# Two tiles move from an eight-bank product to seven-block pairs, and its weights' lows come from adding DMAs

## The chip, the cores and the metric

The kernel runs on one core of one Trainium2 chip. The metric is device time in microseconds (us) of one execution. Engines go by these names: TensorE (PE in the profile; PEld is its weight load), VectorE (DVE), ScalarE (ACT), GpSimd (POOL) and SyncE (SP), which here issues nearly all DMAs.

## The reference

Two pre-norm residual layers over 512 tokens of 1024 features in float32: layer 0 with two kinds of full attention, layer 1 with neighbourhood attention and a relative-position bias. Each is followed by the MLP that this case is about:

```python
def sq_relu_mlp(h, w_up, w_down):
    u = jax.nn.relu(h @ w_up)
    return (u * u) @ w_down
...
for layer in range(DEPTH):                       # DEPTH = 2
    ...
    h = h + sq_relu_mlp(rmsnorm(h, norm_ffn[layer]), ffn_w_up[layer], ffn_w_down[layer])
return rmsnorm(h, final_norm)
```

`w_up` is 1024 x 4096 and `w_down` 4096 x 1024, so the hidden layer has 32 tiles of 128 features by 512 tokens.

## The kernel before

**Three matmuls for one.** A float32 product is made of three matmuls in TensorE's faster 32-bit format: each operand is split into a high part (its rounding, written by ScalarE) and a low part (the operand minus the high part, written by VectorE), and high x high, high x low and low x high are added (`mm3`). So a chunk of weights is loaded by SyncE into a raw buffer, ScalarE writes its high part (`whi`), VectorE its low part (`wlo`). There are 4 raw buffers, 3 high and 3 low ones. Each is 128 x 1024.

**The down product of an MLP** sums over the 32 hidden tiles. `SIZES` says for each MLP how they are divided: (6, 10, 14, 2) in MLP 0 and (6, 10, 12, 4) in MLP 1.
- The first 6 go through a plain product.
- The next 10 go through `product8`: all eight PSUM banks are in use, the loop over weight chunks (one chunk of 128 x 1024 for each hidden tile) is outside, the eight output tiles are inside. The first two chunks are run in two groups of four banks, the last two bank by bank so that banks come free one after another. A chunk is 8 x 3 = 24 matmuls of 512 columns.
- The next 14 (or 12) are kept raw and taken in pairs. `Seven` multiplies 2 x 2 blocks with seven block products for eight (Strassen's way): a chunk is 256 KB of weights, GpSimd makes three block sums of it (`seven_chunk`, L326 to L328), ScalarE the high part (L332) and VectorE the low part (L333), and TensorE runs 7 x 3 = 21 matmuls of 256 columns (L418 to L420). The product runs over four output groups of two tiles (`m`), in each over all pairs: 4 x 7 = 28 chunks in MLP 0, 24 in MLP 1. After each group the blocks are combined by ScalarE and VectorE (L426 to L430) and added to the residual (L1543).
- The last 2 (or 4) go through a plain product again.

The raw pairs' own block sums and their high and low parts (`convert`: `u7.sums`, `u7.split`; VectorE L360, L363, L388, L392, ScalarE L387) are made while `product8` runs, spread over its steps by the counter `at`. In MLP 0 the bias tables of layer 1 are written to HBM in the same place: `bias_rows`, 48 small DMAs (L1457 to L1463), one `next(bias, None)` for each step.

**The order of the weights' work.** Every chunk is planned in a list (`asked`). `weights(i)`, called when TensorE's chunk `i` is about to be emitted, starts the loads of chunks up to `i + LOAD` (5 ahead) and the high and low parts up to `i + AHEAD` (2 ahead). A chunk's steps are a generator: load, then high part, then low part. The three block sums of a `seven_chunk` follow its load directly. A `seven_chunk` takes a slot of the big pool in place of a raw buffer when more than `reserve[0]` slots are free; the pool has `NSLOT` slots of 128 x 1024. `reserve[0]` is 3 in the up product, `NSLOT` (no slots) while `product8` runs, then 1. A scheduler of the framework arranges the emitted instructions on each engine; instructions of one engine start in that order.

Of the kernel before, what the change touches and what calls it, by code (L numbers as in the profile page):

```python
# [8 lines left out]
F32 = mybir.dt.float32  # L9
# [9 lines left out]
P = 128  # L19
# [1 line left out]
FF = 4 * D  # L21
EPS = 1e-6
NEG = -1e30
NSLOT = 30
ROWS = 8
COLS = 64
C_ID, C_I1, C_I2, C_ROPE = 0, 128, 178, 182
# [8 lines left out]
def encoder_kernel(ctx: ExitStack, tc: tile.TileContext, ins, out, dbg=None):  # L36
# [167 lines left out]
    def chunk(parts, nk, ncol, heads=None, eng=None, first=False):  # L204

        raw = wp.tile([P, 1024], F32, tag="raw", bufs=4, name=nm("raw"))
        r3 = raw[:, 0 : nk * ncol].rearrange("p (k n) -> p k n", k=nk)
        for lo, n, src in parts:
            dst = r3[:, :, lo : lo + n]
            if len(src.shape) == 3:  # L210
                SP.dma_start(dst, src)
            else:
                for k in range(nk):
                    SP.dma_start(dst[:, k].rearrange("p (z m) -> p z m", z=src.shape[2]), src[:, k])
        yield
        hi = wp.tile([P, 1024], F32R, tag="whi", name=nm("whi"))
        lo_ = wp.tile([P, 1024], F32R, tag="wlo", name=nm("wlo"))
        m = nk * ncol
        v = lambda t: t[:, 0:m].rearrange("p (k n) -> p k n", k=nk)
        lows = []  # L220

        def low(to, src, high):
            z = lambda: (eng or DVE).tensor_tensor(to, src, f32(high), op=ALU.subtract)  # L223
            if eng:
                z()
            else:
                lows.append(z)

        if heads is None:
            if first:  # L230
                DVE.tensor_copy(hi[:, 0:m], raw[:, 0:m])
            else:
                ACT.activation(hi[:, 0:m], raw[:, 0:m], AF.Copy)  # L233
            low(lo_[:, 0:m], raw[:, 0:m], hi[:, 0:m])
        else:

            na, nb = heads
            hn = ncol // (na + nb)
            r4 = r3.rearrange("p k (h e) -> p k h e", h=hn)
            for e0, n, o in ((0, na, 0), (na, nb, hn * na)):  # L240
                z = [v(t)[:, :, o : o + hn * n].rearrange("p k (h e) -> p k h e", h=hn) for t in (hi, lo_)]
                src = r4[:, :, :, e0 : e0 + n]
                ACT.activation(z[0], src, AF.Copy)
                low(z[1], src, z[0])
        yield v(hi), v(lo_), lows

    def rows(w, k0, nk):
        return w[k0 * P : (k0 + nk) * P, :].rearrange("(k p) n -> p k n", p=P)


    asked, loaded, ready, low_parts = [], [], [], []
    AHEAD, LOAD = 2, 5

    def plan(*spec, make=None):
        asked.append((make or chunk, spec))
# [2 lines left out]
    def preload(n):  # L258
        while len(loaded) < min(n, len(asked)):
            make, spec = asked[len(loaded)]  # L260
            loaded.append(make(*spec))
            next(loaded[-1])

    def weights(i, ahead=AHEAD):
        preload(i + LOAD + 1)
        while len(ready) < min(i + ahead + 1, len(asked)):
            hi, lo, lows = next(loaded[len(ready)])
            ready.append((hi, lo))
            low_parts.append(lows)

            give_low(len(ready) - fixed[0])
        give_low(i + 1)
        return ready[i]
# [45 lines left out]
    def seven_chunk(w, k0, c0):  # L319


        slot = Slot(F32) if len(free) > reserve[0] else None
        raw = slot.t if slot else wp.tile([P, 1024], F32, tag="raw", bufs=4, name=nm("raw"))
        SP.dma_start(raw[:, 0:512].rearrange("p (k n) -> p k n", k=2), rows(w, k0, 2)[:, :, c0 : c0 + 256])
        r = raw.rearrange("p (b n) -> p b n", n=P)
        POOL.tensor_tensor(r[:, 6], r[:, 0], r[:, 1], op=ALU.subtract)  # L326
        POOL.tensor_tensor(r[:, 4:6], r[:, 2:3].to_broadcast([P, 2, P]), r[:, 0:7:6], op=ALU.add)  # L327
        POOL.tensor_tensor(r[:, 7], r[:, 3], r[:, 5], op=ALU.subtract)  # L328
        yield
        hi = wp.tile([P, 1024], F32R, tag="whi", name=nm("whi"))  # L330
        lo = wp.tile([P, 1024], F32R, tag="wlo", name=nm("wlo"))
        ACT.activation(hi[:, 0:896], raw[:, 128:1024], AF.Copy)  # L332
        DVE.tensor_tensor(lo[:, 0:896], raw[:, 128:1024], f32(hi[:, 0:896]), op=ALU.subtract)  # L333
        if slot:
            slot.free()
        yield hi, lo, []
# [154 lines left out]
    def product8(w, first, U, evac, eng=None):  # L491


        nk = len(U)
        ids = [plan([(0, D, rows(w, k, 1))], 1, D, None, eng) for k in first]

        def run():
            banks = group(4) + group(4)

            def one(k, j):  # L500

                wh, wl = (z[:, 0, P * j : P * j + P] for z in weights(ids[k], AHEAD - (k == 1 or k == nk - 1 and j < 7)))
                x = U[k].pair()
                mm3(banks[j], wh, wl, x[:, 0, :], x[:, 1, :], k == 0, k == nk - 1)


            for js in (range(4), range(4, 8)):
                for k in (0, 1):
                    for j in js:
                        one(k, j)  # L510
                        yield MM3
            U[0].free()
            U[1].free()
            for k in range(2, nk - 2):
                for j in range(8):
                    one(k, j)
                    yield MM3
                U[k].free()
            for j in range(8):
                for k in (nk - 2, nk - 1):  # L520
                    one(k, j)
                    yield MM3

                if j < 5:
                    evac(j, banks[j])
            for j in range(5, 8):
                tc.keep_in_program_order(evac(j, banks[j]))
            U[nk - 2].free()
            U[nk - 1].free()

        return run()
# [771 lines left out]

    SIZES = (6, 10, 14, 2), (6, 10, 12, 4)

    def first_product(l):

# [166 lines left out]
    def mlp(l, last=None):  # L1476

        stage, ahead, later = first_product(l)
        reserve[0] = 3
        w = ins["ffn_w_down"][l]
        up4, gens4 = [], []

        def plain_last(k0, V):
            left = list(V)
            gens4.extend(product(w, k0, up4, tiles(512 * c, 512), lambda j, b, c=c: ev(4 * c + j, b), nk=2 * len(V))
                         for c in range(2))

            def beside(m, i):
                if m == 0 and i % 8 == 4 and left:
                    w_ = left.pop(0)
                    for z in range(2):
                        U4.append(Slot())
                        up4.append(U4[-1].pair())
                        split(w_.t[:, S * z : S * z + S], up4[-1])
                    w_.free()

            return beside  # L1500

        U4 = []

        def ev(m, b):
            return DVE.tensor_tensor(hT[:, m, :], hT[:, m, :], b, op=ALU.add)

        U, _, _, (at_u, _), _ = stage(SIZES[l][0])
        up = [s_.pair() for s_ in U]
        gens = [product(w, at_u, up, tiles(512 * c, 512), lambda j, b, c=c: ev(4 * c + j, b)) for c in range(2)]
        ahead()  # L1510
        for c, gen in enumerate(gens):
            for i, _ in enumerate(gen):
                later(c, i)
        for s_ in U:
            s_.free()
        U, R, V, (at_u, at_r), late = stage(*SIZES[l][1:])
        first = [k + z for k in at_u for z in range(2)]
        gen = product8(w, first, U, ev)
        u7 = Seven(2 * len(R))
        ids = [u7.plan(w, 256 * m, at_r) for m in range(4)]  # L1520
        k0 = 32 - 2 * len(V)
        beside = (last or plain_last)(k0, V)
        bias = iter(()) if last else bias_rows()
        reserve[0] = NSLOT
        work, at = convert(u7, R), 0
        for i, _ in enumerate(gen):
            if i in (1, 4, 6):
                next(late, None)
            next(bias, None)

            at += 9 * len(R) + 2
            while at > 0:
                next(work, None)
                at -= 8 * len(U) - 2
        for x in (work, bias):
            for _ in x:
                pass
        reserve[0] = 1
        for m in range(4):

            def evac(w_):
                h2 = hT[:, 2 * m : 2 * m + 2, :]
                DVE.tensor_tensor(h2, h2, w_.t.rearrange("p (z n) -> p z n", z=2), op=ALU.add)  # L1543

            for i, _ in enumerate(u7.run(ids[m], evac)):
                beside(m, i)
        u7.free()
        for gen in gens4:
            for _ in gen:
                pass  # L1550
        for s_ in U4:
            s_.free()
# [487 lines left out]
```

## Time and profile before

| | |
|---|---|
| median of 3 runs | 1158.46 us (1158.25 to 1158.52) |
| the profiled execution: span of its trace | 1157.2 us, 20288 instructions |
| the profiled execution: own time | not listed beside its span; the median is 1.26 us above the span |
| MLP 0: eight-bank product | 450.0 to 505.2 us |
| MLP 0: seven-block product | 505.2 to 574.6 us |
| MLP 1: eight-bank product | 1008.6 to 1064.0 us |
| MLP 1: seven-block product | from 1064.0 us |

Times in the profile count from the start of the span. A row of a windows view gives for each engine the busy time and the number of instructions in that stretch, then the granted clock of TensorE, the mean busy share of the 16 DMA engines, and GB/s. A row of the timeline gives the start, the length, the engine, the line, what is written and read, and in brackets how long the engine was idle before it and what ended that. A row of a group gives the number of instructions, their busy time in us, the mean in ns, and the idle time before them. Matmul lengths in the trace are pipelined, so the pitch from start to start is used for them.

### The profile page before, as it was taken

How to read it: one execution, taken by the hardware profiler on the slowest of the kernel's cores; microseconds unless marked ns; L12 is line 12 of the kernel's file. 1: busy time of each engine (PE TensorE's matmuls, PEld its weight loads, DVE VectorE, ACT ScalarE, POOL GpSimd, SP SyncE). 2: the span in 40 equal slices, each digit the busy share in tenths (PEclk: the TensorE clock that was granted, in tenths of full speed). 3: DMA queues.
4: the chain of work that ended last, by engine and by line, in shares of the span. 5: the costliest groups of instructions: out<-in, count | busy, mean ns of one | idle time of the engine just before them, and what ended most of it. 6: DMA issues, size and time to landing. Idle time of an engine off the chain costs nothing.

```text
span 1157.2 us, 20288 instructions
## 1 busy us (share of the span) xinstructions
PE 1146.8 (99%) x7276; PEld 1021.1 (88%) x7276; DVE 903.0 (78%) x1542; ACT 652.1 (56%) x1115; POOL 577.5 (50%) x708
## 2 busy tenths in 40 slices
PE   9999999999999999999999999999999999999997
PEld 7787888888899999899988998988889999988996
DVE  7887988878978887877685666668987788778675
ACT  6676876755346667433454556555553666743345
POOL 4366252216798882379402232231379889316930
PEclk9999999999999999999999999999999999999999
DMA  8322415122432326523436664443333233432332
GB/s 241 100 74 70 101 51 142 55 67 98 126 93 74 92 83 202 185 92 117 125 98 164 150 174 128 117 109 117 100 120 108 79 89 92 136 102 80 98 106 73
DMA packets 112148, 128.05 MB, mean 111 GB/s; under 512 B 9411, under 2 KB 94576, under 8 KB 112048
## 3 DMA queue, kind: packets, MB, share of 16 engines
q1 hardware_dynamic: 109424, 120.09, 35.4%
q0 software_dynamic: 2304, 6.31, 2.3%
q8 instruction: 57, 0.93, 0.4%
q14 instruction: 43, 0.35, 0.1%
q10 hardware_dynamic: 320, 0.36, 0.1%
HBM read 104.32 MB, written 6.29 MB: 96 GB/s over the span
## 4 chain that ended last, share of the span: by engine, by line
PE 96%; DVE 2%; DMA 1%; issue 1%; ACT 0%; POOL 0%; DVEq 0%; POOLq 0%
PE mm L573 9%; PE mm L575 9%; PE mm L574 9%; PE mm L418 4%; PE mm L420 4%; PE mm L419 4%; PE s L1097 3%; PE t L418 3%; PE t L420 3%; PE t L419 3%; PE o L1085 3%; PE s L573 3%; PE s L574 3%; PE s L575 3%; PE s L418 2%; PE s L420 2%
## 5 line engine op out<-in xcount | busy, mean ns | idle before, releaser
L573 PE MATMUL mm<-a,whi 128*128 128x512 f32 x440 | 178.6, 407 | 0.2
L332 ACT ACTIVATE whi<-a 128x896 fp32r<-128x896 f32 x105 | 99.7, 951 | 132.5 <-POOL a L328 39.2
L574 PE MATMUL mm<-a,whi 128*128 128x512 f32 x440 | 173.5, 394 | 0.0
L575 PE MATMUL mm<-a,wlo 128*128 128x512 f32 x440 | 173.5, 395 | 0.0
L333 DVE TENSOR_TENSOR wlo<-a,whi 128x896 fp32r<-128x896 f32 x105 | 133.1, 1272 | 49.2 <-ACT whi L332 46.1
L223 DVE TENSOR_TENSOR wlo<-raw,whi 128x1024 fp32r<-128x1024 f32 (+4 forms) x113 | 131.1, 1164 | 39.0 <-ACT whi L233 38.4
L233 ACT ACTIVATE whi<-raw 128x1024 fp32r<-128x1024 f32 (+3 forms) x116 | 109.1, 942 | 68.4 <-PE s L574 24.0
L418 PE MATMUL mm<-a,whi 128*128 128x256 f32 x410 | 115.1, 281 | 0.0
L420 PE MATMUL mm<-a,wlo 128*128 128x256 f32 x410 | 114.7, 280 | 0.0
L419 PE MATMUL mm<-a,whi 128*128 128x256 f32 x410 | 114.7, 280 | 0.0
L328 POOL TENSOR_TENSOR a<-a 128x128 f32<-128x128 f32 x105 | 102.9, 980 | 8.2
L326 POOL TENSOR_TENSOR a<-a 128x128 f32<-128x128 f32 x105 | 75.8, 722 | 57.3 <-DMA a<-in_ffn_w_up_dram 37.1
L575 PEld LDWEIGHTS mm<-a,wlo 128*128 128x128 f32 x440 | 82.5, 188 | 18.9
L573 PEld LDWEIGHTS mm<-a,whi 128*128 128x128 f32 x440 | 82.7, 188 | 17.6 <-issue 0.6
L574 PEld LDWEIGHTS mm<-a,whi 128*128 128x128 f32 x440 | 82.9, 188 | 15.3 <-DVE a L930 0.2
L327 POOL TENSOR_TENSOR a<-a 128x256 f32<-128x256 f32 x105 | 90.6, 863 | 8.2
L333 DVE TENSOR_TENSOR wlo<-raw,whi 128x896 fp32r<-128x896 f32 x51 | 62.4, 1226 | 35.4 <-ACT whi L332 35.4
L1683 POOL TENSOR_SCALAR p<-p,ti 128x256 f32<-128x256 f32 x64 | 35.6, 567 | 104.7 <-DVE ti L1682 91.5
L1105 POOL TENSOR_SCALAR p<-p,ti 128x512 f32<-128x512 f32 x64 | 45.0, 705 | 85.7 <-DVE ti L1104 63.6
L418 PE MATMUL t<-a,whi 128*128 128x256 f32 x296 | 83.1, 281 | 0.0
L419 PE MATMUL t<-a,whi 128*128 128x256 f32 x296 | 82.8, 280 | 0.0
L420 PE MATMUL t<-a,wlo 128*128 128x256 f32 x296 | 82.8, 280 | 0.0
(427 smaller groups left out, 3492.9 us busy)
## 6 DMA issues: line engine op xcount, KB each, us to landing
a<-in_ffn_w_up_dram SPq DMA_DIRECT2D x78, 256.0 KB
raw<-in_ffn_w_down_dram SPq DMA_DIRECT2D x38, 512.0 KB
raw<-in_od_w_qkv_dram SPq DMA_DIRECT2D x64, 128.0 KB
a<-in_ffn_w_down_dram SPq DMA_DIRECT2D x27, 256.0 KB
raw<-in_ffn_w_up_dram SPq DMA_DIRECT2D x26, 256.0 KB
raw<-in_ffn_w_down_dram SPq DMA_DIRECT2D x25, 256.0 KB
raw<-in_ffn_w_up_dram SPq DMA_DIRECT2D x12, 512.0 KB
a<-a SPq DMA_DIRECT2D x18, 256.0 KB
```

Source lines behind the costliest of these rows:

```text
L223: z = lambda: (eng or DVE).tensor_tensor(to, src, f32(high), op=ALU.subtract)
L233: ACT.activation(hi[:, 0:m], raw[:, 0:m], AF.Copy)
L327: POOL.tensor_tensor(r[:, 4:6], r[:, 2:3].to_broadcast([P, 2, P]), r[:, 0:7:6], op=ALU.add)
L328: POOL.tensor_tensor(r[:, 7], r[:, 3], r[:, 5], op=ALU.subtract)
L332: ACT.activation(hi[:, 0:896], raw[:, 128:1024], AF.Copy)
L333: DVE.tensor_tensor(lo[:, 0:896], raw[:, 128:1024], f32(hi[:, 0:896]), op=ALU.subtract)
L418: PE.matmul(o, wh, x[:, 0], start=kp == 0 and n in (0, 1, 3, 5), stop=False, skip_group_check=True)
L419: PE.matmul(o, wh, x[:, 1], start=False, stop=False, skip_group_check=True)
L420: PE.matmul(o, wl, x[:, 0], start=False, stop=kp == self.np - 1, skip_group_check=True)
L573: PE.matmul(o, wh, xh, start=first, stop=False)
L574: PE.matmul(o, wh, xl, start=False, stop=False)
L575: PE.matmul(o, wl, xh, start=False, stop=last)
```

## The change

- `SIZES` becomes (6, 8, 16, 2) and (6, 8, 14, 4): two hidden tiles of each MLP go from `product8` to the seven-block product, as one more pair (32 and 28 chunks).
- In `product8`, chunks from the third on are made by the new `summed_chunk`: ScalarE writes minus the raw chunk, rounded, into the low buffer; a DMA that GpSimd issues adds the chunk to it once more from HBM; ScalarE then writes the high part. VectorE has no part in it. The low buffers become 4.
- A new function `begin` emits the second step of `summed_chunk` (at most 3 chunks ahead) and the block sums of `seven_chunk` in the order of the list, so that GpSimd gets its adding DMAs and its block sums in that order.
- `bias_rows` is advanced twice in each step of `product8`.
- `reserve[0]` after `product8` is 3, not 1; `NSLOT` is 32, not 30; the scratch for descriptors of GpSimd's DMAs is set to 2048.

The lines after L254 move: the adding DMA is L256, the block sums become L355 to L357, high and low part of a `seven_chunk` L361 and L362, its matmuls L447 to L449, `mm3` L603 to L605.

```diff
@@
-NSLOT = 30
+NSLOT = 32
@@
         hi = wp.tile([P, 1024], F32R, tag="whi", name=nm("whi"))
-        lo_ = wp.tile([P, 1024], F32R, tag="wlo", name=nm("wlo"))
+        lo_ = wp.tile([P, 1024], F32R, tag="wlo", bufs=4, name=nm("wlo"))
@@
+    def summed_chunk(parts, nk, ncol, heads=None, eng=None):
+
+        raw = wp.tile([P, 1024], F32, tag="raw", bufs=4, name=nm("raw"))
+        v = lambda t: t.rearrange("p (k n) -> p k n", k=nk)
+        (o, n, src), = parts
+        SP.dma_start(v(raw), src)
+        yield
+        lo_ = wp.tile([P, 1024], F32R, tag="wlo", bufs=4, name=nm("wlo"))
+        ACT.activation(lo_, raw, AF.Copy, scale=-1.0)
+        POOL.dma_start(v(lo_), src, accum_op=ALU.add)
+        yield
+        hi = wp.tile([P, 1024], F32R, tag="whi", name=nm("whi"))
+        ACT.activation(hi, raw, AF.Copy)
+        yield v(hi), v(lo_), []
@@
-    AHEAD, LOAD = 2, 5
+    AHEAD, SUM, LOAD = 2, 3, 5
+    begun = [0]
@@
+    def begin(i):
+        while begun[0] < len(loaded):
+            make = asked[begun[0]][0]
+            if make is summed_chunk and begun[0] > i + SUM:
+                break
+            if make in (summed_chunk, seven_chunk):
+                next(loaded[begun[0]])
+            begun[0] += 1
+
     def weights(i, ahead=AHEAD):
-        preload(i + LOAD + 1)
+        while len(loaded) < min(i + LOAD + 1, len(asked)):
+            preload(len(loaded) + 1)
+            begin(i)
+        begin(i)
@@ seven_chunk
         r = raw.rearrange("p (b n) -> p b n", n=P)
+        yield
         POOL.tensor_tensor(r[:, 6], r[:, 0], r[:, 1], op=ALU.subtract)
@@
-        lo = wp.tile([P, 1024], F32R, tag="wlo", name=nm("wlo"))
+        lo = wp.tile([P, 1024], F32R, tag="wlo", bufs=4, name=nm("wlo"))
@@ product8
-        ids = [plan([(0, D, rows(w, k, 1))], 1, D, None, eng) for k in first]
+        ids = [plan([(0, D, rows(w, k, 1))], 1, D, None, eng, make=chunk if n < 2 else summed_chunk)
+               for n, k in enumerate(first)]
@@
-    SIZES = (6, 10, 14, 2), (6, 10, 12, 4)
+    SIZES = (6, 8, 16, 2), (6, 8, 14, 4)
@@ mlp
             next(bias, None)
+            next(bias, None)
@@
-        reserve[0] = 1
+        reserve[0] = 3
@@
-    nc = _bacc.Bacc("TRN2", target_bir_lowering=False, num_devices=1)
+    nc = _bacc.Bacc("TRN2", target_bir_lowering=False, num_devices=1, dynamic_dma_scratch_size=2048)
```

## The prediction

> **What bounds the kernel now.** I read the page first (span, busy times, chain), then the windows view cut at the stage borders of the two MLPs, then the timeline at those borders.
>
> ```profile
> span 1157.2 us, 20288 instructions
> PE 1146.8 (99%) x7276; PEld 1021.1 (88%) x7276; DVE 903.0 (78%) x1542; ACT 652.1 (56%) x1115; POOL 577.5 (50%) x708
> ...
> PE 96%; DVE 2%; DMA 1%; issue 1%; ACT 0%; POOL 0%; DVEq 0%; POOLq 0%
> ```
>
> TensorE is the bound: it is busy 1146.8 of 1157.2 us and carries 96% of the chain. Time can be won by fewer matmul cycles or lost by letting TensorE wait. The stages that the change touches are these (microseconds, then busy time of each engine):
>
> ```profile
> core 0: us, PE busy (x) PEld busy (x) DVE busy (x) ACT busy (x) POOL busy (x), PEclk, DMA share, GB/s
> 450.00:505.10 55.10, 55.10 (x242) 45.03 (x241) 46.61 (x70) 24.27 (x35) 17.76 (x23) 1.00 0.56 177
> 505.20:574.60 69.40, 69.40 (x589) 69.29 (x588) 48.41 (x48) 27.96 (x33) 52.99 (x62) 1.00 0.35 111
> 1008.60:1063.90 55.30, 55.30 (x242) 45.05 (x241) 45.63 (x65) 23.18 (x33) 22.48 (x28) 1.00 0.33 104
> 1064.00:1122.00 58.00, 58.00 (x493) 57.62 (x492) 40.37 (x42) 25.04 (x31) 38.61 (x44) 1.00 0.35 107
> ```
>
> The rows are, in order: the eight-bank product of MLP 0, its seven-block product, and the same two in MLP 1. TensorE is never idle in any of them, at a granted clock of 1.00. So taking work off VectorE there gains nothing by itself. In the seven-block product of MLP 0, GpSimd works 52.99 of 69.40 us on the block sums, and it is done before the end; that is the engine to watch.
>
> **TensorE's own work.** MLP 0's eight-bank product has 10 chunks of 24 matmuls: 55.2 us (450.0 to 505.2) / 240 = 0.2300 us each; MLP 1's 55.4 / 240 = 0.2309. The seven-block product of MLP 0 has 28 chunks of 21 matmuls: 69.4 / 588 = 0.1180 us each, 2.48 us a chunk. Two tiles move from the first to the second: 48 matmuls of 512 columns go, 84 of 256 columns come. MLP 0: -48 x 0.2300 = -11.04, +84 x 0.1180 = +9.91, together -1.13 us. MLP 1 with the same price of a seven-block matmul: -11.08 + 9.91 = -1.17. Sum -2.30 us, which is 0.2% of the time; 0.2% (2.3 us) is also about what a measurement of this kernel can tell from no change. No more can come from matmuls.
>
> **The eight-bank product: adding DMAs for VectorE's lows.** Six of eight chunks in each MLP lose a VectorE subtraction and get a ScalarE write of minus the raw chunk, a GpSimd-issued DMA of 512 KB that adds the chunk from HBM, and the usual high part. No such DMA stands in the trace; the nearest rows are these:
>
> ```profile
> a<-a POOLq DMA_DIRECT2D x16, 256.0 KB, 3.7
> L1591 POOL DMA_DIRECT2D a<-a x16: 512/525/640, 610.6 to 755.0; - x16
> DMA to landing us min/median/max: 2.8/3.7/4.0
> L223 DVE TENSOR_TENSOR wlo<-raw,whi 128x1024 fp32r<-128x1024 f32 x9 | 11.5, 1280 | 5.5 <-ACT whi L233 5.5
> L233 ACT ACTIVATE whi<-raw 128x1024 fp32r<-128x1024 f32 x8 | 8.4, 1055 | 4.1 <-PE s L574 4.0
> L388 DVE TENSOR_TENSOR a<-a,a 128x512 fp32r<-128x512 f32 (+1 forms) x21 | 13.6, 673 | 0.7 <-ACT a L387 0.5
> L388 DVE TENSOR_TENSOR a<-sc,a 128x512 fp32r<-128x512 f32 x7 | 5.3, 761 | 0.0
> L360 DVE TENSOR_TENSOR sc<-a 128x512 f32<-128x512 f32 x7 | 5.1, 722 | 0.0
> L392 DVE TENSOR_TENSOR a<-a 128x256 f32<-128x256 f32 x7 | 3.4, 485 | 0.2
> L363 DVE TENSOR_TENSOR a<-a,sc 128x256 f32<-128x256 f32 x7 | 3.4, 485 | 0.2
> ```
>
> VectorE: converting seven pairs takes 13.6 + 5.3 + 5.1 + 3.4 + 3.4 = 30.8 us, 4.4 a pair. Of its 46.6 us, about eight lows go (-10.2) and one pair comes (+4.4): 40.8 us in a stage that shrinks to 44.2. That is 92%, where it was 85%; cover is thinner but still there. ScalarE gets six more writes of 1.06 us, 6.3 us in all, on 24.3 of 55.
>
> The deadline is the last chunk's low. The high part of chunk 7 in the list must wait for a free buffer of three, so its minus-write, queued on ScalarE behind that, comes only when chunk 4 has left TensorE: 450.0 + 4 x 5.52 = 472.1, then 2 x 1.06 for the two writes, then 0.53 to issue: 474.7. The landing is bounded below by 2.8 us and above by twice 4.0 for twice the bytes: 477.5 to 482.7. The last two chunks run bank by bank, so TensorE wants the last low at 450.0 + 6 x 5.52 + 5 x 0.23 = 484.3. It lands 1.6 to 6.8 us early; I take a cost of 0.3 us, between nothing and the rival below. A gain is excluded, since TensorE never waits in this stage.
>
> [...]
>
> The bias writes of MLP 0 go out at twice the rate in program order, so they end before the block sums' loads rather than between them; they fill the queue of SyncE earlier and cost it nothing more. Chunks that had landed before 450 are not touched.
>
> **The seven-block product: where the cost comes from.** After the change its chunks may use only the four raw buffers (a slot of the pool is given only when more than three are free, and none are), with one exception in MLP 1. Before, nearly half of this stage's chunks in MLP 0 took slots (the lows that read `a`, by groups of instructions in the stage's window), and their sums were made far ahead. Below them are timeline rows of ScalarE, TensorE, VectorE, SyncE's queue and GpSimd at the start of the stage:
>
> ```profile
> L333 DVE TENSOR_TENSOR wlo<-raw,whi 128x896 fp32r<-128x896 f32 x15 | 18.4, 1233 | 9.6 <-ACT whi L332 9.6
> L333 DVE TENSOR_TENSOR wlo<-a,whi 128x896 fp32r<-128x896 f32 x12 | 14.9, 1254 | 9.4 <-ACT whi L332 6.6 <-PE o L419 2.7
> ...
> 504.52 0.96 ACT L332 ACTIVATE whi<-raw 128x896 fp32r<-128x896 f32 x1 [5.34 <-PE s L574]
> 505.18 0.28 PE L418 MATMUL s<-a,whi 128*128 128x256 f32 x1
> 505.50 1.16 DVE L333 TENSOR_TENSOR wlo<-raw,whi 128x896 fp32r<-128x896 f32 x1 [1.60 <-ACT whi L332]
> 506.69 6.26 SPq L324 DMA_DIRECT2D raw<-in_ffn_w_down_dram  x4
> 509.40 1.38 POOL L326 TENSOR_TENSOR raw<-raw 128x128 f32<-128x128 f32 x1 [2.42 <-DMA raw<-in_ffn_w_down_dram]
> ```
>
> The low of the second chunk ends at 506.66 (its high part waits until 504.52 for TensorE to leave the eight-bank product); that frees a raw buffer, the next load goes out at 506.69 and its sums start at 509.40. In the kernel before this load is for the ninth chunk. After the change there are only four raw buffers, so the load that follows the second chunk's low is the sixth chunk's: three chunks, 7.4 us of lead, are gone. From there on GpSimd must keep TensorE's pace. What it can do, from the end of the stage, where it works back to back:
>
> ```profile
> 556.22 0.46 POOL L326 TENSOR_TENSOR a<-a 128x128 f32<-128x128 f32 x1
> ...
> 557.57 1.20 POOL L328 TENSOR_TENSOR a<-a 128x128 f32<-128x128 f32 x1
> 558.73 0.46 POOL L326 TENSOR_TENSOR raw<-raw 128x128 f32<-128x128 f32 x1
> ...
> 562.59 1.33 POOL L328 TENSOR_TENSOR a<-a 128x128 f32<-128x128 f32 x1
> 567.34 0.95 ACT L332 ACTIVATE whi<-raw 128x896 fp32r<-128x896 f32 x1 [1.65 <-PE s L419]
> 568.33 1.09 DVE L333 TENSOR_TENSOR wlo<-raw,whi 128x896 fp32r<-128x896 f32 x1 [1.47 <-ACT whi L332]
> 572.22 0.28 PE L418 MATMUL mm<-a,whi 128*128 128x256 f32 x1
> ```
>
> An undisturbed chunk takes 558.73 - 556.22 = 2.51 us, already more than TensorE's 2.48. The 20 chunks from 509.40 to 562.59 + 1.33 = 563.92 took 54.52, or 2.73 each: evacuations on VectorE stretch some by 1 to 2 us, 4.3 us in all over 20 x 2.51. The last sums ended 3.4 us before ScalarE took them, so the kernel before came out just right.
>
> After: 27 chunks (6th to 32nd) stand behind that load. On the clock of before, with the same 4.3 us of stretching, they end at 509.40 + 27 x 2.51 + 4.3 = 581.5; at 2.73 each, 583.1. High and low part take 2.1 us more (567.34 to 569.42): 583.6 to 585.2. TensorE would start its 32nd chunk at 505.18 + 31 x 2.48 = 582.1. It waits 1.5 to 3.1 us in all; I take 2.4, since a late evacuation can also hold up a low and with it a buffer. Ends: nothing (at 2.51 throughout, 579.3), and 5.4 us at MLP 1's pace, next.
>
> ```profile
> 1064.03 0.28 PE L418 MATMUL s<-a,whi 128*128 128x256 f32 x1
> 1065.64 5.94 SPq L324 DMA_DIRECT2D raw<-in_ffn_w_down_dram  x4
> 1070.71 0.80 POOL L326 TENSOR_TENSOR raw<-raw 128x128 f32<-128x128 f32 x1 [4.78 <-DMA raw<-in_ffn_w_down_dram]
> 1108.81 1.19 POOL L328 TENSOR_TENSOR a<-a 128x128 f32<-128x128 f32 x1
> 1122.84 0.28 PE L418 MATMUL mm<-a,whi 128*128 128x256 f32 x1
> ```
>
> In MLP 1 the last 14 chunks took 1110.00 - 1070.71 = 39.3 us, 2.81 each, while TensorE, with the final turn's transposes in between, needs (1122.84 - 1064.03) / 23 = 2.56 a chunk. After the change the first load that waits is the seventh's (one slot). 22 chunks at 2.81 from 1070.71 end at 1132.5, with high and low at 1134.6; TensorE wants the 28th at 1064.03 + 27 x 2.56 = 1133.1: 1.5 us late. If that first load lands in 2.7 us as in MLP 0, and not in 5.1, nothing is late. I take 0.5.
>
> **Sum.** -2.30 + 0.3 + 2.4 + 0.5 = +0.9 us. The profiled execution's span is 1157.2 us, 1.26 below the median of 1158.46; that rest stays, so 1158.46 + 0.9 = 1159.4 us. More slots (32 for 30) and the smaller scratch of GpSimd's descriptors shift some loads elsewhere; nothing there is priced, as TensorE is busy all but 10.4 us of the whole span: at most 1 us either way.
>
> **Rivals.**
> - *The sums keep up.* If the four buffers suffice (2.51 us a chunk, no stretching), only the matmuls count: 1158.46 - 2.30 = 1156.2. For it: 4.3 us of stretching came with evacuations, and those become fewer per chunk (one in eight, not one in seven). Against: 2.51 is above 2.48 and the lead is gone. Half of this case is over the 0.2%.
> - *GpSimd is the bound of both seven-block products.* Place: the block sums (L326 to L328, new L355 to L357). At 2.81 us a chunk MLP 0's 27 take 75.9: sums at 585.3, low at 587.4, 5.3 us late; MLP 1 1.5. 1158.46 - 2.30 + 5.3 + 1.5 + 0.3 = 1163.3. It is slower by over 0.2% once the waits together pass 4.6 us, that is from about 2.77 us a chunk.
> - *The adding DMAs come late.* In MLP 0 they share the DMA engines with 48 bias writes (share 0.56 in that stage against 0.33 in MLP 1), and each reads as much again as the load. If landing takes 12 us, three times the longest row, the last low comes at 486.7, 2.4 us late, and TensorE pays all of it, perhaps for a second chunk too: about 3 us, 1162.4. [...]
> - *The conversions fall behind.* VectorE at 92% would bring the seven-block product's first operands late. Small, and inside the third case's range.
>
> **Chances.** Forecast 0.45 (1157.2 to 1161.5), sums keep up 0.22, GpSimd bounds both 0.18, DMAs late 0.15. Faster by over 0.2%: half of the second, and 0.05 of the first: 0.16. Slower: 0.10 of the first, 0.17 of the third, 0.13 of the fourth: 0.40. Within: 0.44. The range runs from half a microsecond under the second case, 1155.7, to the third, 1163.4.
>
> **What would show it.** In the profile after: the eight-bank products should last 44.2 and 44.3 us without a gap of TensorE; the seven-block product of MLP 0 should start with no wait, and from its middle on the high part (new L361) should wait for GpSimd's last sum (new L357) and no longer for TensorE; TensorE's gaps there should add up to 1.5 to 3.1 us. I am wrong if the high parts still wait for TensorE at the end of that stage (sums keep up), if gaps of TensorE stand in the eight-bank product behind a low that a DMA wrote, or if the time changed in a stage outside the MLPs.

## The result, and the profile after

The changed kernel takes 1172.82 us (median; 1172.19 to 1173.26) against 1158.49 of the kernel before: a ratio of 1.012 (95% interval 1.0106 to 1.0134), 14.3 us slower. The forecast was 1159.4 us with a range up to 1163.4. The profiled execution took 1172.19 us, 1.9 more than its span.

The page of the changed kernel, its span, busy times and chain:

```profile
span 1170.3 us, 20576 instructions
...
PE 1149.5 (98%) x7348; PEld 1024.3 (88%) x7348; DVE 894.0 (76%) x1544; ACT 668.4 (57%) x1135; POOL 597.6 (51%) x744
...
PE 79%; DVE 6%; POOL 5%; DMA 3%; issue 3%; SPq 2%; ACT 2%; DVEq 0%; POOLq 0%; ACTq 0%
```

TensorE still bounds the kernel, but its share of the chain falls from 96% to 79%: VectorE, GpSimd, transfers and SyncE's queue (SPq) now stand in it. The windows view of the same stages as before, in the same order, and then the end of MLP 0's eight-bank product cut in three:

```profile
core 0: us, PE busy (x) PEld busy (x) DVE busy (x) ACT busy (x) POOL busy (x), PEclk, DMA share, GB/s
450.73:506.66 55.93, 48.09 (x194) 38.24 (x193) 40.76 (x69) 29.87 (x46) 14.85 (x19) 0.91 0.70 184
506.66:587.31 80.65, 79.63 (x673) 79.22 (x672) 52.15 (x53) 31.91 (x37) 67.27 (x81) 1.00 0.35 114
1022.79:1067.32 44.53, 44.26 (x195) 35.97 (x194) 41.88 (x65) 29.08 (x43) 15.43 (x23) 1.00 0.61 150
1067.32:1138.28 70.96, 70.96 (x606) 70.96 (x604) 48.75 (x49) 30.25 (x37) 56.52 (x66) 1.00 0.37 120
...
484.00:490.70 6.70, 0.60 (x3) 0.18 (x1) 2.72 (x6) 0.49 (x1) 0.98 (x2) 0.92 0.97 173
490.70:500.00 9.30, 7.55 (x17) 5.53 (x18) 4.95 (x6) 3.36 (x5) 4.04 (x5) 0.51 0.63 184
500.00:506.60 6.60, 6.60 (x30) 5.43 (x30) 6.60 (x11) 1.23 (x2) 5.32 (x8) 1.00 0.12 40
```

Three of the four stages are near what was worked out; the loss is in the first. It should have shrunk by 11.04 us and lasts 55.93, as long as before with two tiles more. In its end TensorE is idle for 6 us (484.0 to 490.7) and then runs at half clock for 9 us (0.51). The spans of the two kernels differ by 13.15 us, by stage (a stage reaches from TensorE's first matmul in it to the first of the next):

| stage | before | after | worked out from matmuls alone | left over |
|---|---|---|---|---|
| up product of MLP 0 | 128.29 | 129.02 | 0 | +0.73 |
| eight-bank product, MLP 0 | 55.19 | 55.94 | -11.04 | +11.79 |
| seven-block product, MLP 0 | 69.52 | 80.65 | +9.91 | +1.22 |
| between the MLPs (layer 1's attention mostly) | 305.49 | 306.76 | 0 | +1.27 |
| up product of MLP 1 | 128.44 | 128.72 | 0 | +0.28 |
| eight-bank product, MLP 1 | 55.42 | 44.52 | -11.08 | +0.18 |
| seven-block product, MLP 1 | 61.28 | 70.96 | +9.91 | -0.23 |
| end | 31.88 | 32.06 | 0 | +0.18 |

The timeline of the changed kernel at the end of that stage, all engines in order of time (start, length, engine, line; in brackets the idle time before and what ended it):

```profile
465.52 0.86 POOL L256 DMA_DIRECT2D wlo<-in_ffn_w_down_dram  x1 [1.13 <-DMA bx<-a]
466.59 0.85 SPq L252 DMA_DIRECT2D raw<-in_ffn_w_down_dram  x1
...
469.06 1.04 ACT L255 ACTIVATE wlo<-raw 128x1024 fp32r<-128x1024 f32 x1
...
476.74 0.38 SPq L352 DMA_DIRECT2D raw<-in_ffn_w_down_dram  x1
476.78 1.06 ACT L255 ACTIVATE wlo<-raw 128x1024 fp32r<-128x1024 f32 x1 [1.77 <-DMA raw<-in_ffn_w_down_dram]
...
481.06 0.45 POOL L355 TENSOR_TENSOR raw<-raw 128x128 f32<-128x128 f32 x1 [14.69 <-ACT a L416]
482.48 0.79 POOL L357 TENSOR_TENSOR raw<-raw 128x128 f32<-128x128 f32 x1
483.22 1.77 POOL L256 DMA_DIRECT2D wlo<-in_ffn_w_down_dram  x2
485.36 1.85 SPq L1493 DMA_DIRECT2D bx<-a  x1
490.74 0.79 PE L605 MATMUL s<-p,wlo 128*128 128x512 f32 x1 [6.14 <-DMA wlo<-in_ffn_w_down_dram]
494.09 0.80 PE L605 MATMUL s<-p,wlo 128*128 128x512 f32 x1 [1.70 <-DMA wlo<-in_ffn_w_down_dram]
494.27 0.63 ACT L416 ACTIVATE a<-sc 128x512 fp32r<-128x512 f32 x1 [9.78 <-DMA bx<-a]
```

Read it from the wait back. TensorE waits 6.14 us at 490.74 and 1.70 us at 494.09 for lows that an adding DMA wrote. Both DMAs were issued at 483.22, in one stretch of 1.77 us (x2). The minus-write of the first of the two had been done since 469.06 + 1.04 = 470.10: its DMA stood 13 us in GpSimd's queue behind the block sums of the first seven-block chunk (481.06 to 483.27). GpSimd itself was idle for 14.69 us before those. The bracket there names ScalarE's L416, but the sums also need their load, and SyncE issued that only at 476.74; between 464 and 487 SyncE's queue is a row of bias writes (L1487, L1491, L1493), one each 0.6 to 1.1 us, some up to 2.3. The load of the eighth chunk, issued among them at 466.59, is waited for until 476.78, and so its minus-write comes 3.6 us later than the 473.2 of the prediction's sum (0.73 of that is the later start of the stage).

A second path runs beside it, in the last row: ScalarE's conversion of the raw pairs waits 9.78 us for a bias write to land. That conversion writes into big-pool slots which the bias tables held.

The adding DMAs themselves, by the view of one source line:

```profile
L256 POOL DMA_DIRECT2D wlo<-in_ffn_w_down_dram x12: 856/872/1184, 446.9 to 1050.6; - x12
DMA to landing us min/median/max: 5.3/7.0/10.2
```

Issue takes 0.86 to 1.18 us (0.53 was taken) and landing 5.3 to 10.2 us (2.8 to 8.0 was taken). In MLP 0 alone the median is 7.9, in MLP 1 6.1.

### The profile page after: what moved, and what is told of

It reads as the page before. It is cut to its first block, busy times and chain, and to the rows that moved or that the text cites. A ratio compares the mean times of both kernels' runs of the same rounds, so it can differ in the third digit from the quotient of the medians.

```text
span 1170.3 us, 20576 instructions
## 1 busy us (share of the span) xinstructions
PE 1149.5 (98%) x7348; PEld 1024.3 (88%) x7348; DVE 894.0 (76%) x1544; ACT 668.4 (57%) x1135; POOL 597.6 (51%) x744
## 4 chain that ended last, share of the span: by engine, by line
PE 79%; DVE 6%; POOL 5%; DMA 3%; issue 3%; SPq 2%; ACT 2%; DVEq 0%; POOLq 0%; ACTq 0%
PE mm L603 8%; PE mm L604 8%; PE mm L605 8%; PE s L1127 3%; PE mm L449 3%; PE mm L447 3%; PE mm L448 3%; PE o L1115 3%; PE t L1102 2%; PE t L447 2%; PE t L449 2%; PE t L448 2%; PE s L605 2%; POOL raw L357 2%; PE s L603 2%
## 5 line engine op out<-in xcount | busy, mean ns | idle before, releaser
L603 PE MATMUL mm<-a,whi 128*128 128x512 f32 x428 | 173.9, 407 | 0.2
L362 DVE TENSOR_TENSOR wlo<-a,whi 128x896 fp32r<-128x896 f32 x103 | 128.1, 1247 | 54.6 <-ACT whi L361 54.3
L604 PE MATMUL mm<-a,whi 128*128 128x512 f32 x428 | 168.9, 395 | 0.0
L605 PE MATMUL mm<-a,wlo 128*128 128x512 f32 x428 | 168.9, 396 | 0.0
L361 ACT ACTIVATE whi<-a 128x896 fp32r<-128x896 f32 x103 | 97.8, 949 | 105.3 <-PE o L604 27.5
L233 ACT ACTIVATE whi<-raw 128x1024 fp32r<-128x1024 f32 (+3 forms) x100 | 92.2, 924 | 68.1 <-PE s L604 19.4
L223 DVE TENSOR_TENSOR wlo<-raw,whi 128x1024 fp32r<-128x1024 f32 (+4 forms) x97 | 110.6, 1145 | 24.1 <-ACT whi L233 19.7
L449 PE MATMUL mm<-a,wlo 128*128 128x256 f32 x430 | 120.5, 280 | 1.0 <-DVE wlo L362 1.0
L447 PE MATMUL mm<-a,whi 128*128 128x256 f32 x430 | 120.7, 281 | 0.0
L448 PE MATMUL mm<-a,whi 128*128 128x256 f32 x430 | 120.4, 280 | 0.0
L362 DVE TENSOR_TENSOR wlo<-raw,whi 128x896 fp32r<-128x896 f32 x61 | 73.2, 1203 | 49.7 <-ACT whi L361 49.3
L361 ACT ACTIVATE whi<-raw 128x896 fp32r<-128x896 f32 x61 | 57.9, 953 | 86.4 <-POOL raw L357 54.5
L356 POOL TENSOR_TENSOR a<-a 128x256 f32<-128x256 f32 x103 | 98.6, 957 | 8.0
L355 POOL TENSOR_TENSOR a<-a 128x128 f32<-128x128 f32 x103 | 60.2, 584 | 81.6 <-DMA a<-in_ffn_w_up_dram 75.7
L357 POOL TENSOR_TENSOR a<-a 128x128 f32<-128x128 f32 x103 | 96.5, 937 | 8.0
L605 PEld LDWEIGHTS mm<-a,wlo 128*128 128x128 f32 x428 | 80.3, 188 | 18.4
L603 PEld LDWEIGHTS mm<-a,whi 128*128 128x128 f32 x428 | 80.4, 188 | 17.1 <-issue 1.3
L447 PE MATMUL t<-a,whi 128*128 128x256 f32 x312 | 87.6, 281 | 0.0
L448 PE MATMUL t<-a,whi 128*128 128x256 f32 x312 | 87.4, 280 | 0.0
```

Of the source, the lines that this page charges most:

```text
L447: PE.matmul(o, wh, x[:, 0], start=kp == 0 and n in (0, 1, 3, 5), stop=False, skip_group_check=True)
L448: PE.matmul(o, wh, x[:, 1], start=False, stop=False, skip_group_check=True)
L449: PE.matmul(o, wl, x[:, 0], start=False, stop=kp == self.np - 1, skip_group_check=True)
L603: PE.matmul(o, wh, xh, start=first, stop=False)
L604: PE.matmul(o, wh, xl, start=False, stop=False)
L605: PE.matmul(o, wl, xh, start=False, stop=last)
```

## The experiments

All of them start from the changed kernel, except e5. The table has each one's median with its ratio to the kernel before on the same chip (1158.86 to 1158.92 us; 1158.49 for the row after), and the four stages from the profile, cut as above. e5, e6, e9 and e10 have the sizes of before, so their eight-bank product is 55.2 us at best.

| run | us | ratio (95%) | eight-bank, MLP 0 | seven-block, MLP 0 | eight-bank, MLP 1 | seven-block, MLP 1 |
|---|---|---|---|---|---|---|
| after | 1172.82 | 1.012 (1.0106 to 1.0134) | 55.94 | 80.65 | 44.52 | 70.96 |
| e1 order held | 1170.24 | 1.010 (1.0083 to 1.0117) | 47.14 | 85.96 | 44.41 | 70.96 |
| e2 bias early | 1164.67 | 1.0048 (1.0033 to 1.0063) | 44.16 | 81.76 | 44.41 | 70.92 |
| e3 VectorE's lows | 1168.01 | 1.0079 (1.0064 to 1.0094) | 44.14 | 84.71 | 44.46 | 72.85 |
| e4 early and held | 1163.80 | 1.0046 (1.0031 to 1.0061) | 45.04 | 82.00 | 44.22 | 70.92 |
| e5 before, bias twice | 1158.75 | 1.000 (0.999 to 1.0009) | 55.15 | 69.58 | 55.15 | 61.29 |
| e6 adding DMAs only | 1182.17 | 1.0198 (1.0179 to 1.0217) | 76.16 | 69.34 | 56.92 | 61.17 |
| e7 bias first | 1161.46 | 1.0024 (1.0014 to 1.0035) | 44.18 | 81.35 | 44.05 | 70.97 |
| e8 bias first, slots | 1161.11 | 1.0021 (1.0011 to 1.003) | 44.98 | 81.32 | 44.05 | 70.96 |
| e9 adding DMAs, held | 1169.56 | 1.009 (1.0072 to 1.0108) | 62.08 | 70.82 | 55.86 | 61.16 |
| e10 adding DMAs, bias first | 1163.37 | 1.0041 (1.0025 to 1.0057) | 55.63 | 69.36 | 56.55 | 61.00 |
| e11 bias first, VectorE's lows | 1168.83 | 1.0081 (1.0066 to 1.0096) | 45.12 | 84.84 | 44.77 | 72.85 |
| e12 the same, five raw buffers | 1167.60 | 1.0072 (1.0057 to 1.0087) | 45.77 | 83.46 | 44.83 | 72.85 |

### e1: GpSimd's order held

```diff
-        POOL.dma_start(v(lo_), src, accum_op=ALU.add)
+        tc.keep_in_program_order(POOL.dma_start(v(lo_), src, accum_op=ALU.add))
...
+        held = tc.keep_in_program_order
-        POOL.tensor_tensor(r[:, 6], r[:, 0], r[:, 1], op=ALU.subtract)
+        held(POOL.tensor_tensor(r[:, 6], r[:, 0], r[:, 1], op=ALU.subtract))
...
```

> The changed kernel with one edit: the adding DMAs and the block sums keep the program's order on GpSimd, so that the first seven-block chunk's sums stand behind the last two adding DMAs and no longer ahead of them. Theory A (those two DMAs were issued at 483.2 because the sums stood ahead of them on GpSimd and waited for a load that SyncE sent late): the seventh chunk's DMA goes out at about 470.5 and the eighth's at about 478, the wait of 6.3 us at the seventh chunk goes, 1 to 2 us at the eighth stay, and with the waits the low clock behind them: about 1162 us (1160 to 1164). Theory B (adding DMAs take 7 to 10 us to land and come late whatever stands ahead of them on GpSimd): the wait shrinks by less than 3 us, 1169 or more.

Measured: 1170.24 us, 2.6 less than after. Timeline of e1 (its lines after L356 are one further down):

```profile
478.29 0.86 POOL L256 DMA_DIRECT2D wlo<-in_ffn_w_down_dram  x1 [7.24 <-ACT wlo L255]
482.96 0.46 POOL L356 TENSOR_TENSOR raw<-raw 128x128 f32<-128x128 f32 x1 [3.81 <-DMA raw<-in_ffn_w_down_dram]
485.59 0.50 PE L606 MATMUL s<-p,wlo 128*128 128x512 f32 x1 [0.33 <-DMA wlo<-in_ffn_w_down_dram]
491.31 0.64 ACT L417 ACTIVATE a<-sc 128x512 fp32r<-128x512 f32 x1 [7.55 <-DMA bx<-a]
497.85 0.36 PE L448 MATMUL s<-a,whi 128*128 128x256 f32 x1 [2.21 <-DVE hT L1536]
```

The last adding DMA goes out at 478.29, ahead of the sums, and TensorE waits 0.33 us for its low and no more. The eight-bank product falls to 47.14 us: at least 8.8 of the 11.8 us lost there were GpSimd's order. But most of it is given back. ScalarE still waits for a bias write (7.55 us), VectorE's evacuations come late behind the conversions, and TensorE waits for them three times: 2.21 us before the first seven-block matmul (it counts into the eight-bank product as the stages are cut), 0.51 and 0.94 us soon after. From 499.54 to 506.25, that is from before the third of these waits, the matmuls run at a pitch of 0.21 us and not 0.118, and the seven-block product takes 85.96 us. So there are two paths, and holding the order cures one.

### e2 and e4: the bias writes in the up product, without and with the held order

```diff
-        def stage(n, raw=0, more=0):
+        def stage(n, raw=0, more=0, extra=iter(())):
...
+                    if i >= 0 and u % 4 == 0:
+                        next(extra, None)
...
-        U, R, V, (at_u, at_r), late = stage(*SIZES[l][1:])
+        bias = iter(()) if last else bias_rows()
+        U, R, V, (at_u, at_r), late = stage(*SIZES[l][1:], extra=bias)
...
-        bias = iter(()) if last else bias_rows()
```

> The changed kernel with one edit: the 48 bias writes of MLP 0 are issued during the up product and not during the eight-bank product; the order on GpSimd stays as it was. Theory A: the loads of the chunks and of the first seven-block chunk go out 10 us or more earlier, its sums do not hold up the adding DMAs, and MLP 0's eight-bank product looks like MLP 1's (44.5 us): about 1161 us (1159.5 to 1163). Theory B: with the DMA engines less loaded landing takes 5 us and not 7 to 10, the last low still comes some 2 to 4 us late: 1164 to 1167. Theory C (the order on GpSimd alone is at fault, SyncE's queue is not): no change, 1172.

> The changed kernel with both edits: bias writes during the up product, and GpSimd's order held. Theory A: both eight-bank products without a wait over 0.5 us; what is left of the loss is the seven-block product of MLP 0, 1 to 2 us, against a gain of 2.3 us in matmuls: about 1159 us (1157 to 1161). Theory B: 1163 or more.

Measured: 1164.67 and 1163.80 us; the intervals overlap almost wholly. Against e1, e4 has the bias writes moved and nothing else, and its seven-block product takes 82.00 us, 4.0 less: the second path is the bias writes' too. With the bias writes away, the eight-bank product of MLP 0 takes the 44.16 us of its matmuls, GpSimd's order untouched (e2; the 45.04 us of e4 hold two waits of 0.5 us at the start of the stage, behind a high part and a low of VectorE). So the order costs only where the loads behind it are late. In the windows view of e2 (its eight-bank product, then its up product):

```profile
454.00:498.00 44.00, 44.00 (x194) 35.92 (x193) 41.15 (x68) 28.93 (x45) 14.70 (x19) 1.00 0.62 155
322.40:454.00 131.60, 129.60 (x1093) 128.84 (x1093) 95.19 (x108) 83.58 (x103) 104.39 (x127) 1.00 0.39 118
```

The first row has no gap left. The second shows the price of the place chosen: the up product takes 131.58 us, 3.3 more than before, and TensorE is idle for 131.60 - 129.60 = 2.0 us of it. In e4, with the same place, it takes 130.09 us.

### e3: VectorE's lows in place of the adding DMAs

```diff
-        ids = [plan([(0, D, rows(w, k, 1))], 1, D, None, eng, make=chunk if n < 2 else summed_chunk)
+        ids = [plan([(0, D, rows(w, k, 1))], 1, D, None, eng, make=chunk)
```

> The changed kernel without the adding DMAs: all eight chunks' lows by VectorE, as in the kernel before; the rest of the change stays (sizes, bias writes at twice the rate, slots). Theory A: nothing on GpSimd is in the path of the eight-bank product any more, so no wait of more than 1 us there: about 1161 us (1159 to 1163). Theory D (VectorE cannot carry eight lows and eight pairs in 44.2 us): waits at lows or at the start of the seven-block product, 3 to 6 us: 1164 to 1167.

Measured: 1168.01 us. The eight-bank product is whole again (44.14 us) with the bias writes still at twice the rate, so the loss of 11.8 us needs the adding DMAs. But the seven-block products take 84.71 and 72.85 us: there VectorE is late. e11 shows the same without the bias writes beside it.

### e5: the kernel before with the bias writes at twice the rate

```diff
             next(bias, None)
+            next(bias, None)
```

> The kernel before with one edit: the bias writes of MLP 0 are advanced twice in each step of the eight-bank product. Sizes, slots and VectorE's lows stay. Theory A2 (the double rate by itself does no harm as long as nothing in the path stands behind the writes; it hurts only with the adding DMAs and with conversions that take over the bias tables' slots): 1158.5 us, within 1 us. Theory E (the double rate by itself delays chunk loads and conversions): 1161 us or more.

Measured: 1158.75 us, ratio 1.000 (0.999 to 1.0009). The doubled rate alone costs nothing in the kernel before.

### e6, e9 and e10: adding DMAs at the sizes of before

e6: the adding DMAs with the sizes, the bias rate and the reserve of before.

```diff
-    SIZES = (6, 8, 16, 2), (6, 8, 14, 4)
+    SIZES = (6, 10, 14, 2), (6, 10, 12, 4)
...
-            next(bias, None)
...
-        reserve[0] = 3
+        reserve[0] = 1
```

> The changed kernel with the sizes of before (ten chunks in the eight-bank product, 28 and 24 in the seven-block products), bias writes at the single rate, and reserve 1 as before: what is left of the change is the adding DMAs, GpSimd's order and the slots. On GpSimd one chunk's sums stand ahead of the ninth chunk's adding DMA and three chunks' sums ahead of the tenth's. Theory A (block sums whose loads stand behind bias writes hold up the adding DMAs): a wait of 3 to 8 us near the end of MLP 0's eight-bank product and none over 1 us in MLP 1's: 1163 us (1161 to 1168). Theory F (adding DMAs harmless at the single rate): 1158.5 us, within 1.

e9 is e6 with the held order of e1; e10 is e6 with the bias writes in the plain product, as the diff of e7 below.

> As the run with the adding DMAs alone (sizes of before, single rate of the bias writes), with GpSimd's order held: all eight adding DMAs of MLP 0 stand ahead of the first block sums. Theory A: of the 21 us lost in that eight-bank product the part that comes from sums standing ahead goes: it lasts 55.5 to 60 us, not 76.2, and the kernel takes 1161 to 1166 us, not 1182. MLP 1's, which lost 1.5 us, loses under 0.5. Theory B (landing is what is late): 70 us or more, 1176 or more.

> As the run with the adding DMAs alone (sizes of before), with the bias writes moved into the first plain down product; GpSimd's order is the scheduler's, with one chunk's sums ahead of the ninth adding DMA and three more ahead of the tenth. Theory A: without bias writes ahead of the block sums' loads in SyncE's queue the sums run early, and the eight-bank product takes 55.2 to 57 us: 1159 to 1161.5 us. Theory C (the order on GpSimd alone is at fault): 70 us or more there, 1174 or more.

Measured: 1182.17, 1169.56 and 1163.37 us. The eight-bank product of MLP 0 takes 76.16, 62.08 and 55.63 us where its matmuls need 55.2. So the same two causes act here, at the old rate of the bias writes and at the old sizes: it is not the doubled rate, and not the extra pair. The timeline of e6 on GpSimd:

```profile
482.04 0.86 POOL L256 DMA_DIRECT2D wlo<-in_ffn_w_down_dram  x1 [7.92 <-DMA raw<-in_ffn_w_down_dram]
496.97 0.45 POOL L355 TENSOR_TENSOR raw<-raw 128x128 f32<-128x128 f32 x1 [14.06 <-DMA raw<-in_ffn_w_down_dram]
498.92 0.90 POOL L256 DMA_DIRECT2D wlo<-in_ffn_w_down_dram  x1 [0.17 <-issue]
...
510.56 0.89 POOL L256 DMA_DIRECT2D wlo<-in_ffn_w_down_dram  x1
```

Here the bracket at the first sum names the load itself: GpSimd is idle for 14.06 us waiting for it, with an adding DMA behind. TensorE's waits of e6 in this stage, and of e9:

```profile
PE s L605 <- DMA wlo<-in_ffn_w_down_dram: 17.5, 2, 9.3
```

```profile
PE s L606 <- DMA wlo<-in_ffn_w_down_dram: 4.2, 1, 4.2
```

17.5 us with the order left to the scheduler, 4.2 with the order held.

### e7 and e8: the bias writes in the first plain product

The plain product of the first six tiles comes between the up product and the eight-bank product. e7 puts the writes there, and all are out before `product8`.

```diff
+        bias = iter(()) if last else bias_rows()
...
+                next(bias, None)
+                next(bias, None)
...
+        for _ in bias:
+            pass
...
-        bias = iter(()) if last else bias_rows()
```

> The changed kernel with one edit: the 48 bias writes are issued during MLP 0's first plain down product, where the seven-block up product does not yet run, so that neither the up product (which lost 3.3 us in the run with early writes) nor the eight-bank product shares its time with them. Theory A: up product 128.5 to 129 us, eight-bank product 44.2 us, seven-block product of MLP 0 81.7 us (2.3 us of waits on GpSimd's sums), about 1 us lost between it and the next layer: 1160.5 us (1159.5 to 1162).

> As the run with the bias writes in the first plain down product, and reserve[0] after the eight-bank product is 2 and not 3, by which six chunks of the seven-block products take a slot instead of one. If the waits in MLP 0's seven-block product (2.3 us) come from lead that is lost for want of buffers, each chunk in a slot gives GpSimd up to 2.5 us of lead: waits under 0.5 us where the slots fall in MLP 0, 1159 us (1158 to 1160.5). If they come from GpSimd's pace against VectorE alone, no change against that run.

Measured: 1161.46 us, and 1161.11 with `reserve[0] = 2` beside it (e8), which makes no difference. But of the six chunks that then take a slot only one lies in MLP 0's seven-block product (L361 reads `a` once there and five times in MLP 1's), so e8 does not tell what more buffers would gain in MLP 0. 11.4 us of the 14.3 are gone. The windows of e7, its eight-bank and seven-block product of MLP 0:

```profile
451.45:495.63 44.18, 44.18 (x194) 36.09 (x193) 41.39 (x69) 29.18 (x45) 14.83 (x19) 1.00 0.62 154
495.63:576.98 81.35, 79.68 (x673) 79.25 (x672) 52.43 (x54) 31.93 (x37) 67.43 (x81) 1.00 0.36 113
```

```profile
479.11 0.88 POOL L256 DMA_DIRECT2D wlo<-in_ffn_w_down_dram  x1
```

The last adding DMA still stands behind block sums and goes out at 479.11, late by the prediction's 474.7, and the stage has no gap. The 2.6 us by which e7 is still above the 1158.86 us of the kernel before are +2.22 in the spans: -2.30 are matmuls, +1.9 the seven-block product of MLP 0 (81.35 against 69.52 + 9.91 = 79.43), +3.0 the opening, the two up products and the stretch between the MLPs (+0.66, +0.81, +0.32 and +1.20), and -0.4 the other stages.

### e11 and e12: bias writes first, and VectorE's lows

e11 is e7 with the edit of e3. e12 has five raw and three low buffers in place of four and four:

```diff
-        raw = wp.tile([P, 1024], F32, tag="raw", bufs=4, name=nm("raw"))
+        raw = wp.tile([P, 1024], F32, tag="raw", bufs=5, name=nm("raw"))
...
-        lo_ = wp.tile([P, 1024], F32R, tag="wlo", bufs=4, name=nm("wlo"))
+        lo_ = wp.tile([P, 1024], F32R, tag="wlo", name=nm("wlo"))
```

> As the run with bias writes in the first plain down product (1161.5 us), with VectorE's lows in place of the adding DMAs. It tells what the adding DMAs bring where nothing disturbs them. Theory D (VectorE then has about 43.5 us of work in 44.2 and falls behind by the end of the eight-bank product): seven-block product of MLP 0 83.5 to 85 us, not 81.4, that of MLP 1 72 to 73, not 71: 1164 to 1167. Theory G (VectorE was late in the earlier run with its lows only because of the bias writes' slots): the same time as with adding DMAs, 1161.5, within 1.

> As the run with bias writes first and VectorE's lows, with five raw buffers (and three low buffers, as in the kernel before). If the 2 us of waits of the seven-block product of MLP 0 come from lead that four raw buffers do not allow, one more buffer gives up to 2.5 us of lead: 1.5 to 2.5 us less there than in that run. If VectorE's lateness sets it, no change.

Measured: 1168.83 and 1167.60 us. Against e7 the adding DMAs are worth 7.4 us. The windows of e11 and TensorE's waits in both stages:

```profile
451.41:496.53 45.12, 44.50 (x194) 36.02 (x193) 43.94 (x69) 23.30 (x36) 10.84 (x14) 1.00 0.27 88
496.53:581.37 84.84, 80.73 (x673) 79.49 (x672) 56.23 (x59) 33.07 (x38) 68.32 (x83) 1.00 0.34 108
```

```profile
PE s L449 <- DVE wlo L362: 1.8, 2, 1.0
PE t L447 <- DVE hT L1535: 1.1, 1, 1.1
```

VectorE is busy 43.94 of 45.12 us, and TensorE then waits for VectorE's lows and evacuations at the start of the seven-block product. The fifth raw buffer shortens that product by 1.4 us (84.84 to 83.46), and its total by 1.2, which the two intervals do not separate.

No run beat the kernel before. The expected times held in e5, e7 and e8. e1, e2, e3, e4, e6, e9, e10 and e11 came out above the range of the theory whose mechanism their stages showed, by 1.0 us (e3) to 14.2 us (e6). For e12 either 1.5 to 2.5 us less or no change was expected in the seven-block product; it is 1.4 us less.

## Why the prediction was wrong, point by point

- **The matmuls: right.** MLP 1's eight-bank product lasts 44.52 us (44.3 worked out), its seven-block product 70.96 (71.2 by the pitch); in MLP 0 e2, e3 and e7 give 44.14 to 44.18 (44.2).
- **The step that failed: "then 0.53 to issue: 474.7".** The step lets an adding DMA go out as soon as its minus-write is done. In the changed kernel the last two went out one behind the other from 483.22 on. Three things had been left out. First, what stands ahead on GpSimd: the prediction took program order, adding DMAs before block sums, for the order on the engine; the scheduler had put a chunk's block sums between. e1 shows their price, 8.8 us of the stage. Second, the loads: those sums and the eighth chunk's minus-write wait for loads that SyncE issues among the bias writes; with the writes elsewhere (e2, e7) the same order costs nothing. Third, the clock. After the wait sixteen matmuls (490.74 to 499.38) ran at a pitch of 0.43 us and not 0.23: 3.2 us on top of about 8 us of waiting. The rival "adding DMAs come late" had the place, but priced it at 3 us by the landing alone (its 1162.4 still holds the forecast's 0.3 beside them).
- **The landing: mis-sized.** "477.5 to 482.7" had 2.8 to 8.0 us; it is 5.3 to 10.2, and 5.3 to 8.8 even in e7, where no bias writes stand beside the adding DMAs. The minimum is nearly twice the bound below.
- **The bias writes: "cost it nothing more" was wrong with adding DMAs and right without.** In e5 they cost nothing at twice the rate; e6, with adding DMAs at the old rate, loses 21.0 us in the stage; e7 and e10, with the writes elsewhere, lose none and 0.4. Only the two together are a loss of this size. Why the kernel before bore the bias writes without a wait is argued, not shown: its loads may have had enough slack, where an adding DMA makes a load's time count twice, once for the minus-write and once through GpSimd's queue.
- **The slots: a wait that was not seen.** The conversion of raw pairs takes over slots of the bias tables, and the faster stage reaches that point before the writes have landed (9.78 us of ScalarE after, 7.55 in e1). In e1 it costs 4.0 us of the seven-block product (against e4).
- **VectorE's cover: right, and worth more than was thought.** VectorE at 92% was forecast; it is 41.39 of 44.18 us in e7, 94%. Without the adding DMAs it would have been 97% (e11), and the next stage late by 3.5 us in MLP 0 and 1.9 in MLP 1. The adding DMAs are needed for the smaller stage; the prediction saw only what they cost.
- **The seven-block products: right in kind, a little too dear.** 2.4 us (1.5 to 3.1) was forecast for MLP 0; e7 has 1.9, and the changed kernel 1.2, under that range. For MLP 1 0.5 was taken, between nothing and 1.5; it is nothing. (The end "5.4 us at MLP 1's pace" comes to 5.3 by the prediction's own numbers, as its rival has it.) The sign that was named is there too, in the waits of e7 in that stage:

```profile
ACT whi L361 <- POOL raw L357: 32.1, 20, 2.4
PE mm L449 <- DVE wlo L362: 1.0, 1, 1.0
```

  The high part waits for GpSimd's last sum in 20 chunks, for 32.1 us of ScalarE, and TensorE feels it in a few waits of a microsecond or less behind a low. The sign is not as clean as it was named: seven high parts still wait for TensorE, 12.8 us in all, two of them as late as 563.77 and 567.12. The rival "GpSimd is the bound of both" (5.3 us late) is excluded. What stretches the sums was put down to evacuations, and that is not shown: in the trace of before the six sums at L326 that take 1.31 to 1.38 us run beside VectorE's lows (L333), while the six beside the combining of a group (L427 to L430) take 0.46 to 0.47.
- **"At most 1 us either way" elsewhere: too little.** In e7 the opening, the up products and the stretch between the MLPs cost 3.0 us together, in after 2.3. They are what keeps e7 above the kernel before: without them its span would be 0.8 below.

Left open: what makes those 2 to 3 us outside the changed stages (no run has the 32 slots, the smaller scratch or the new order of emission alone); whether the eighth chunk's load is late because of its place in SyncE's queue or because the DMA engines were full then (a share of 1.06 from 467 to 472 us); and why e6 and e10 lose 1.5 and 1.1 us in MLP 1's eight-bank product, where no bias writes stand. Part of that last loss is again GpSimd's order: TensorE waits 0.67 and 0.54 us there for a low that an adding DMA wrote, and in e9, with the order held, there is no such wait and the loss is 0.45 us.

## What to carry to other kernels

When work moves to a queue that a scheduler orders, read the order on the engine before pricing the step, and follow what stands ahead of it to its own inputs: a DMA that is ready waits as long as the least ready instruction before it (13 us in the changed kernel). Price a step that depends on a load by the loads of its stage, with everything else that the same queue issues then; a stage without gaps shows no slack, neither how much there is nor that there is none. And give a wait of TensorE of several microseconds more than its length: around the waits of 4.24 us (e9) and of 6.14 and 1.70 us (after) the clock fell, which cost some 2 and 3 us more, while single waits of 0.69 and 0.98 us in e7's seven-block product left it at 1.00.

## What the runs showed of the hardware

- **The clock around a wait.** By the granted clock, the changed kernel ran at half rate from 489.58 to 499.82, e9 from 498.60 to 505.43, e1 from 499.50 to 506.32 and e6 from 500.09 to 520.57 (with waits of 9.3 and 8.1 us). In the changed kernel it fell 5.0 us into the wait of 6.14 us, and another wait of 1.70 us lies inside; from 494.09 the matmuls ran without a gap, and the pitch went from 0.43 to about 0.24 us at 500.06, 6 us later. In e9 it fell 2.05 us into a single wait of 4.24 us, and full rate was back 4.6 us after that wait. A wait of 0.33 us in e1 left it alone. The waits of 2.21 and 0.51 us there, with seven matmuls between and behind them, brought half pitch for 6.8 us, and the wait of 0.94 us came inside that time. Half rate began in e1 1.65 us after the wait of 2.21 us had ended. Full rate was back 5.7 us (changed kernel), 4.6 (e9) and 5.2 (e1) after the end of the last of these waits. How much idle time brings half rate is not shown.
- **An adding DMA of 512 KB** takes 0.86 to 1.18 us of GpSimd to issue (medians of 0.86 to 0.88) and 5.3 to 10.4 us to land in the changed kernel, e1, e2, e6, e7, e9 and e10 (e9 the longest).
- **The format of the three matmuls** is the faster one by the trace of before: the four plain float32 matmuls at L911, 512 columns with two output rows, start 0.43 us apart at a granted clock of 1.00 (1.88 us for the four from 106.36), against 0.23 us for a matmul of 512 columns in `mm3`.
